# The mean squares and the prompt's attention in the free PSUM columns of the score tiles, in a hybrid backbone step on one Trainium2 core

## The chip, the cores and the metric

The kernel runs on one core of a Trainium2 chip. The metric is the device time of one execution in microseconds (us). The five engines of a core each work through a program of their own, in order: PE (TensorE, matmuls and transposes), DVE (VectorE), ACT (ScalarE), POOL (GpSimd) and SP (SyncE, which here only issues DMAs). Matmul results land in PSUM, which has eight banks of 512 fp32 columns per partition.

## The reference

Two layers of a hybrid backbone with 1,024 sample tokens, 128 prompt tokens and a model width of 1,024. One input projection of each layer yields q, k, v and gate of four attention heads and the inputs of a Fourier and a gMLP branch. The attention is differential and ends in a norm over each head's 128 outputs:

```python
s = einsum('bhqmd,bhkmd->bhmqk', q, k) * HEAD_DIM ** -0.5      # m = 0, 1
p = softmax(s, axis=-1)
a = p[:, :, 0] - lam * p[:, :, 1]
o = einsum('bhqk,bhke->bhqe', a, v)
o = o * rsqrt(mean(o ** 2, axis=-1) + RMS_EPS) * subln_w * (1 - lam_init)
```

Sample queries see 128 cached and 1,024 own keys (1,152 in all); the prompt's 128 queries see the prompt's 128 keys alone. Then `mixed = o * silu(gate)` and the branches go through an output projection and a layer norm.

## The kernel before, in words

**The stages.** Each layer projects its inputs (line 386, PSUM tiles `z`, matmuls of 128x384), works through the attention, the gMLP and the Fourier branch, and ends in the output projection (`y`, line 1013). The attention does not wait for all projections: the projections of later heads and of the branches are cut into small steps and are put between the steps of the attention by the generator `fill`, so that TensorE has work while ACT and DVE do the softmax.

**The attention.** `attention` (line 695) has one iteration per query tile of 128 queries, eight tiles in each of four heads; tile i of head h is step n = 8h + i. An iteration has four steps on TensorE, with projections behind each: the scores for m = 0 and for m = 1 (`score`, line 632: six matmuls into a tile `S`, DVE's maximum `nm` at line 640, ACT's exponential `P` at line 642), every second time the product with the values for two earlier tiles (`values`, line 658: 27 matmuls into `pv`), and the nine transposes of the previous tile's probabilities (`transpose`, line 646: `T`, copied by ACT at line 655 to `a`, the rest of the precision by DVE at line 656). Between scores and transposes, `softmax_diff` (lines 583 to 585) joins both exponentials on DVE and POOL.

**PSUM.** `S`, `T` and `pv` share the tag "S": two slots of three banks each. A score fills columns 0 to 383 of each of its three banks; columns 384 to 511 stay empty. A new tile of this tag takes over the slot of the tile two allocations earlier, once all of that tile's readers are done. All other results (`z`, `vt`, and the prompt's small tiles) share the tag "mm": two slots of one bank.

**The norm.** `values` squares `pv` on ACT (`sq`, line 589). One step of projections later `finish_o` lets TensorE form the mean of the squares (a matmul with a matrix of 1/128, line 594) into the other half of the bank that holds `pv`, DVE multiplies `pv` into `gs` (line 595), ACT reads the mean (`msq`, line 598), takes a logarithm and an exponential (lines 599, 600), POOL multiplies three times (601 to 603), and DVE finishes (604). The slot of `pv` is free after line 598.

**The prompt's attention.** `prompt` (line 670) is a generator of five steps, started after the first `values` of a head and served by a `Stream` at one step per step of the attention: two scores (`sp`, line 678, with a maximum and an exponential `Pp` each, lines 679 and 680), the softmax, a transpose (`atp`, line 685, copied by ACT at 687), the product (`pvp`, line 690) and its norm. Every tile of it takes a slot of the tag "mm", between two `z`.

**The order.** TensorE's order is the order in which the program is written (`manual_schedule`). The other engines are ordered by a scheduler, with the attention's instructions ahead (`high_priority`).

Of the kernel before, what the change touches and what calls it, by code (L numbers as in the profile page):

```python
# [12 lines left out]
AF = mybir.ActivationFunctionType  # L13
ALU = mybir.AluOpType
AX = mybir.AxisListType
# [4 lines left out]
SEQ_S = 1024  # L20
# [10 lines left out]

PACE = 2
SHARE = [0.75, 1.25, 1, 1]
# [17 lines left out]

X_TAGS = {"wr": ("wraw", "woraw", "wada", "tabr", "mr", "ba"), "z": ("zz", "sh", "gt", "vT", "gmt", "gmg", "fot", "vs", "bd", "pqp", "ws", "kc", "vc", "Pp", "modacc"), "Q": ("Q", "bdr", "wsr", "h32"),
          "sq": ("sq", "wft", "dftp", "msq", "bds", "cb")}
X_BUFS = {"wr": 2, "z": 3, "Q": 2, "sq": 3, "X": 2}
# [8 lines left out]
def backbone_step(ctx, tc, xs, xp, cT, w_ada, b_ada, w_in, w_out, ckT, cv, lamv, wf, wsT, bsT,  # L63
# [527 lines left out]

    def finish_o(l, o, ms, sq, n, gs, sl):

        pe.matmul(ms, lhsT=onesm, rhs=sq[:, :n], start=True, stop=True)
        dve.scalar_tensor_tensor(gs[:, sl], o, subs[:, l:l + 1], gs[:, sl], op0=ALU.mult, op1=ALU.mult)

        m = tX([128, 256], "msq")[:, :n]
        act.activation(m, ms, AF.Identity, bias=epsr)
        act.activation(sq[:, :n], m, AF.Ln)
        act.activation(sq[:, :n], sq[:, :n], AF.Exp, scale=-0.5)  # L600
        pool.tensor_tensor(m, m, sq[:, :n], op=ALU.mult)
        pool.tensor_tensor(m, m, sq[:, :n], op=ALU.mult)
        pool.tensor_tensor(gs[:, sl], gs[:, sl], sq[:, :n], op=ALU.mult)
        dve.scalar_tensor_tensor(gs[:, sl], m, 3.0, gs[:, sl], op0=ALU.subtract, op1=ALU.mult)


    class Head:
# [23 lines left out]

        def score(self, Q, i, m, zz):
            S, K = psS(), self.K
            ql = slice((i % 2) * 128, (i % 2) * 128 + 128)

            for e, q in enumerate((Q[:, m, ql], qlo[i % 2][:, m])):
                for n in range(3):
                    pe.matmul(S[:, n, :CH], lhsT=q, rhs=K[:, m, n * CH:(n + 1) * CH], start=e == 0, stop=e == 1)  # L638
            nm = small([128, 1], "nm", 4)
            dve.tensor_reduce(nm, S[:, :, :CH], axis=AX.XY, op=ALU.max, negate=True)  # L640
            P = tP(name="P")
            act.activation(P.rearrange("p (c k) -> p c k", c=3), S[:, :, :CH], AF.Exp, bias=nm,  # L642
                           accum_out=zz[:, m:m + 1])
            return P

# [12 lines left out]
        def values(self, p):  # L658
            pv = psS((128, 2, 256), "pv")
            for kt in range(NT):  # L660
                for e, (a, b) in enumerate(((0, 0), (0, 1), (1, 0))):
                    pe.matmul(pv[:, 0, :], lhsT=self.V[:, a, kt, :], rhs=self.A[:, b, kt, :],  # L662
                              start=kt == 0 and e == 0, stop=kt == 8 and e == 2)
# [6 lines left out]
        def prompt(self):  # L670

            l = self.l
            nm = small([128, 2], "nmp", 2)
            zz = small([128, 2], "zzp", 2)
            P = tX([128, 2, 128], "Pp")
            for m in range(2):
                S = psM((128, 128), "sp")
                pe.matmul(S, lhsT=self.qp[:, m], rhs=self.kp, start=True, stop=True)
                dve.tensor_reduce(nm[:, m:m + 1], S, axis=AX.X, op=ALU.max, negate=True)
                act.activation(P[:, m], S, AF.Exp, bias=nm[:, m:m + 1], accum_out=zz[:, m:m + 1])  # L680
                yield 0.5 * PACE
            softmax_diff(l, P[:, 0], P[:, 1], zz, "p")
            yield 0.5 * PACE
            pt = psM((128, 128), "atp")
            pe.transpose(pt, P[:, 0], ident)
            aT = P[:, 1]
            act.activation(aT, pt, AF.Copy)
            yield 0.5 * PACE
            pv = psM((128, 2, 128), "pvp")
            pe.matmul(pv[:, 0], lhsT=self.vp, rhs=aT, start=True, stop=True)  # L690
            sq = square_o(pv[:, 0], 128)
            yield 0.5 * PACE
            finish_o(l, pv[:, 0], pv[:, 1], sq, 128, self.gs, slice(SEQ_S, TOK))

    def attention(l, fill):
# [3 lines left out]
        done = None  # L699
        side = Stream()  # L700
        for n in range(8 * H + 2):
            h, i = min(n // 8, H - 1), n % 8
            if n < 8 * H:
                if i == 0:
                    fill.until((l, U_K + h), (l, U_Q + h), (l, U_V + h))
                    hd = Head(l, h)
                    Qn = hd.pack(0)
# [8 lines left out]
                with tc.high_priority(offset=EARLY):  # L716
                    side.fill(1)
# [5 lines left out]
                with tc.high_priority(offset=EARLY):  # L723
                    side.fill(1)
                yield h, 1
            if done:
                if done[1] == 0:
                    fill.until((l, U_G + done[0].h))
                    done[0].begin_values()
                with tc.high_priority(offset=EARLY):  # L730
                    finish = done[0].values(done[1])
                with tc.high_priority(offset=EARLY):
                    side.fill(1)
                yield h, 2
                with tc.high_priority(offset=EARLY):
                    finish()
                if done[1] == 0:
                    side.gens.append(done[0].prompt())
                if done[1] == 3:
                    with tc.high_priority(offset=EARLY):  # L740
                        side.drain()
                    done[0].store()
                done = None
            if turn:
# [5 lines left out]
                turn = None  # L750
                with tc.high_priority(offset=EARLY):
                    side.fill(1)
                yield h, 3
            if n < 8 * H:
                with tc.high_priority(offset=EARLY):
                    softmax_diff(l, p1, p2, zz, "s")
                turn = hd, i, p1

    TG = [[0, 1], [2, 3], [4, 5], [6, 7], [8]]
# [394 lines left out]
```

## Time and profile before

| | us |
|---|---|
| three runs | 1438.85, 1442.42, 1443.56 |
| their median | 1442.42 |
| the profiled execution, its own time | 1439.59 |
| its span, first to last instruction | 1437.7 |
| PE busy | 1330.9 (93%) |
| POOL, DVE, ACT busy | 793.4 (55%), 907.6 (63%), 746.6 (52%) |
| mean granted TensorE clock | 0.979 |

The span is cut by the program into stages. The attention of layer 0 lies between 96 and 580 us (the heads begin at 96, 191, 294 and 412), that of layer 1 between 807 and 1,262 us. A busy share says how much of the time an engine was at work; a wait says how long it stood and whose signal it got last. A timeline row is one instruction, or a run of like ones, with its start and its length, and, in brackets, how long the engine had stood before it.

### The profile page before, as it was taken

Reading aid. Unit: us, or ns where it says so; the run is one execution under the profiler, and the core shown is the slowest. Engines: PE = TensorE matmul, PEld = TensorE weight load, DVE = VectorE, ACT = ScalarE, POOL = GpSimd, SP = SyncE. Lnnn points to the kernel's source line nnn. Section 1 sums busy time; section 2 is a strip of 40 time slices with the busy share of each in tenths; the row PEclk is TensorE's granted clock in tenths of the full one; section 3 lists DMA queues with packets and bytes.
Section 4 is the critical chain, followed back from the end, with each engine's and each line's share of the span. In section 5 each row is a group of like instructions: output and inputs, shape, how many; then the busy total and the mean of one; then the engine's idle time right before and its main releaser. Section 6 shows DMA issues by size and latency. Waiting matters only on the chain. (4 is left out here: it accounts for less than half of the span.)

```text
span 1437.7 us, 21298 instructions
## 1 busy us (share of the span) xinstructions
PE 1330.9 (93%) x8264; PEld 1236.6 (86%) x8264; DVE 907.6 (63%) x1354; ACT 746.6 (52%) x1380; POOL 793.4 (55%) x723
## 2 busy tenths in 40 slices
PE   6899998889899999999997989989799999999997
PEld 4689998879788998987887989988789999998786
DVE  3646667787877865355785565668775684435576
ACT  3576666557454444353656565755565544435320
POOL 2455657567563446336687676575575343533752
PEclk9999999999999999999999999999999999999999
DMA  9310102211220221363341100112020010126432
GB/s 337 147 49 17 35 18 65 75 46 36 88 76 22 98 74 42 108 211 114 124 161 45 50 19 32 49 44 80 32 65 3 30 47 30 47 78 221 154 133 80
DMA packets 56158, 114.43 MB, mean 80 GB/s; under 512 B 4973, under 2 KB 32493, under 8 KB 55929
## 3 DMA queue, kind: packets, MB, share of 16 engines
q1 hardware_dynamic: 56056, 113.07, 23.7%
q8 instruction: 65, 1.06, 0.3%
q14 instruction: 37, 0.30, 0.1%
HBM read 95.47 MB, written 17.58 MB: 79 GB/s over the span
## 5 line engine op out<-in xcount | busy, mean ns | idle before, releaser
L386 PE MATMUL z<-H,w 128*128 128x384 f32 x2520 | 499.8, 345 | 22.4 <-DVE V L506 5.0
L386 PEld LDWEIGHTS z<-H,w 128*128 128x128 f32 x2520 | 444.9, 193 | 29.0 <-ACT vT L492 4.9
L642 ACT ACTIVATE P<-S,nm 128x1152 f32<-128x1152 f32 x128 | 156.4, 1222 | 118.6 <-DVE nm L640 112.1
L640 DVE TENSOR_REDUCE nm<-S 128x1 f32<-128x1152 f32 x128 | 172.3, 1349 | 40.4 <-PE S L638 39.9
L401 PE MATMUL zt<-whi,H 128*128 128x256 f32 x1152 | 158.7, 285 | 4.8 <-ACT ug L767 3.4
L401 PEld LDWEIGHTS zt<-whi,H 128*128 128x128 f32 x1152 | 147.0, 192 | 7.5 <-ACT ug L767 4.0
L584 POOL TENSOR_SCALAR P<-P,rz,neglam 128x1152 f32<-128x1152 f32 x64 | 86.8, 1356 | 98.3 <-DVE rz L583 87.2
L585 DVE SCALAR_TENSOR_TENSOR P<-P,rz 128x1152 f32<-128x1152 f32 x64 | 105.2, 1643 | 42.3 <-POOL P L584 42.3
L630 POOL TENSOR_TENSOR qlo<-qr,Q 64x128 fp32r<-64x128 f32 x128 | 81.4, 641 | 86.8 <-PE S L638 80.2
L367 POOL TENSOR_TENSOR w<-wraw,w 128x1024 fp32r<-128x1024 f32 x36 | 89.6, 2489 | 65.4 <-ACT w L366 64.9
L638 PE MATMUL S<-K,Q 128*128 128x384 f32 x384 | 93.2, 351 | 21.4 <-DVE a L656 11.0
L662 PE MATMUL pv<-a,V 128*128 128x256 f32 x864 | 109.2, 283 | 3.1 <-ACT P L642 3.1
L662 PEld LDWEIGHTS pv<-a,V 128*128 128x128 f32 x864 | 106.6, 191 | 5.1 <-ACT P L642 5.1
L656 DVE TENSOR_TENSOR a<-T,a 128x1152 fp32r<-128x1152 f32 x64 | 86.6, 1353 | 37.5 <-ACT a L655 37.4
L638 PEld LDWEIGHTS S<-K,Q 128*128 128x128 f32 x384 | 67.6, 194 | 29.8 <-DVE a L656 12.8
L638 PE MATMUL S<-K,qlo 128*128 128x384 f32 x384 | 89.7, 342 | 0.0
L1013 PE MATMUL y<-wob,mx 128*128 128x512 f32 (+1 forms) x342 | 88.3, 385 | 1.5 <-DVE rr L1015 1.5
L655 ACT ACTIVATE a<-T 128x1152 fp32r<-128x1152 f32 x64 | 72.3, 1130 | 28.5 <-PE T L652 28.2
L406 PE MATMUL zt<-wlo,H 128*128 128x256 f32 x576 | 82.7, 284 | 1.1 <-POOL wlo L367 1.1
L1013 PE MATMUL y<-wo,mx 128*128 128x512 f32 (+1 forms) x342 | 81.6, 382 | 0.0
L652 PE MATMUL T<-cs,P 128*128 128x128 f32 x576 | 73.9, 274 | 3.8 <-ACT P L642 3.7
L406 PEld LDWEIGHTS zt<-wlo,H 128*128 128x128 f32 x576 | 74.9, 191 | 1.5 <-POOL wlo L367 1.5
(222 smaller groups left out, 2376.9 us busy)
## 6 DMA issues: line engine op xcount, KB each, us to landing
wraw<-in_w_in_dram SPq DMA_DIRECT2D x52, 512.0 KB, 3.3
wada<-in_w_ada_dram SPq DMA_DIRECT2D x32, 512.0 KB, 3.6
wa<-in_w_ada_dram SPq DMA_DIRECT2D x8, 1024.0 KB, 13.0
woraw<-in_w_out_dram SPq DMA_DIRECT2D x16, 512.0 KB, 3.9
mr<-mix SPq DMA_DIRECT2D x18, 384.0 KB, 3.2
mix<-gs SPq DMA_DIRECT2D x8, 576.0 KB, 3.9
x<-rr SPq DMA_DIRECT2D x9, 512.0 KB, 3.6
xr<-x SPq DMA_DIRECT2D x9, 512.0 KB, 5.3
```

Of the source, the lines that this page charges most:

```text
L367: eng.tensor_tensor(lo, raw, f(hi), op=ALU.subtract)
L386: pe.matmul(z, lhsT=w[:, a, kt, :], rhs=Hc[c][:, b, kt, :], start=n == 0, stop=n == 23)
L401: pe.matmul(z[:, i, :], lhsT=Hc[c][:, a, kt, o:o + 128], rhs=w[0][:, kt, :], start=n == 0, stop=False)
L406: pe.matmul(z[:, i, :], lhsT=Hc[c][:, 0, kt, o:o + 128], rhs=w[1][:, kt, :], start=False, stop=kt == KT - 1)
L584: pool.tensor_scalar(p2, p2, rz[:, 1:2], neglam[:, l:l + 1], op0=ALU.mult, op1=ALU.mult)
L585: return dve.scalar_tensor_tensor(p1, p1, rz[:, 0:1], p2, op0=ALU.mult, op1=ALU.add)
L638: pe.matmul(S[:, n, :CH], lhsT=q, rhs=K[:, m, n * CH:(n + 1) * CH], start=e == 0, stop=e == 1)
L640: dve.tensor_reduce(nm, S[:, :, :CH], axis=AX.XY, op=ALU.max, negate=True)
L642: act.activation(P.rearrange("p (c k) -> p c k", c=3), S[:, :, :CH], AF.Exp, bias=nm, accum_out=zz[:, m:m + 1])
L656: dve.tensor_tensor(lo, T[:, :, 0:3], f(hi), op=ALU.subtract)
L662: pe.matmul(pv[:, 0, :], lhsT=self.V[:, a, kt, :], rhs=self.A[:, b, kt, :], start=kt == 0 and e == 0, stop=kt == 8 and e == 2)
L1013: pe.matmul(z, lhsT=mx[:, a, k, :], rhs=wo[kt][b][:, ns], start=i == 0, stop=i == 23)
```

## The change

Four things are written differently.

- The mean of the squares no longer shares the bank of `pv`. `values` now only squares `pv` and multiplies it into `gs` (`begin_o`); it returns `norm`, and the next iteration's first score calls it behind its six matmuls with the free columns of its tile, `S[:, :, 384:]` (`aside`). The mean is two matmuls of 128 columns, in two banks (`mean_o`). The rest of the norm (`finish_o`) follows behind that score's exponential.
- The prompt's attention is a table of four steps, {2: scores, 4: turn, 5: product, 6: norm}: in iteration i of its head the step's matmuls go into the free columns of the second score's tile, and what reads them follows behind that score's exponential. Both score matmuls, one maximum over both, both exponentials and `softmax_diff` are one step. No tile of the prompt takes a slot of the tag "mm" any more, and `Stream`'s part in it and `PACE` are gone.
- The buffer `Pp` in SBUF moves from the group of `z`'s buffers to that of `sq`.
- The store of a head's `gs` to DRAM is issued one step later, behind the last norm.

```diff
-    def finish_o(l, o, ms, sq, n, gs, sl):
-
-        pe.matmul(ms, lhsT=onesm, rhs=sq[:, :n], start=True, stop=True)
+    def begin_o(l, o, n, gs, sl):
+
+        sq = square_o(o, n)
         dve.scalar_tensor_tensor(gs[:, sl], o, subs[:, l:l + 1], gs[:, sl], op0=ALU.mult, op1=ALU.mult)
+        return sq
+
+    def mean_o(free, sq, n):
+
+        for t in range(n // 128):
+            pe.matmul(free[:, t], lhsT=onesm, rhs=sq[:, t * 128:(t + 1) * 128], start=True, stop=True)
+        return free[:, 0:n // 128]
+
+    def finish_o(ms, sq, n, gs, sl):
+
         m = tX([128, 256], "msq")[:, :n]
-        act.activation(m, ms, AF.Identity, bias=epsr)
+        act.activation(m.rearrange("p (t k) -> p t k", k=128), ms, AF.Identity, bias=epsr)
...
-        def score(self, Q, i, m, zz):
+        def score(self, Q, i, m, zz, aside=None):
...
+            after = aside(S[:, :, CH:]) if aside else None
             nm = small([128, 1], "nm", 4)
             dve.tensor_reduce(nm, S[:, :, :CH], axis=AX.XY, op=ALU.max, negate=True)
...
+            if after:
+                after()
             return P
...
         def values(self, p):
-            pv = psS((128, 2, 256), "pv")
+            pv = psS((128, 256), "pv")
...
-            sq = square_o(pv[:, 0], 256)
-            return lambda: finish_o(self.l, pv[:, 0], pv[:, 1], sq, 256, self.gs, slice(p * 256, (p + 1) * 256))
+            sl = slice(p * 256, (p + 1) * 256)
+            sq = begin_o(self.l, pv, 256, self.gs, sl)
+
+            def norm(free):
+                ms = mean_o(free, sq, 256)
+                return lambda: finish_o(ms, sq, 256, self.gs, sl)
+
+            return norm
...
         def prompt(self):
...
+            def scores(free):
+                P = self.P = tX([128, 2, 128], "Pp")
+                for m in range(2):
+                    pe.matmul(free[:, m], lhsT=self.qp[:, m], rhs=self.kp, start=True, stop=True)
+
+                def after():
...
+                    dve.tensor_reduce(nm, free[:, 0:2], axis=AX.X, op=ALU.max, negate=True)
+                    for m in range(2):
+                        act.activation(P[:, m], free[:, m], AF.Exp, bias=nm[:, m:m + 1], accum_out=zz[:, m:m + 1])
+                    softmax_diff(self.l, P[:, 0], P[:, 1], zz, "p")
+                return after
+
+            def turn(free):
+                pe.transpose(free[:, 0], self.P[:, 0], ident)
+
+                return lambda: act.activation(self.P[:, 1], free[:, 0], AF.Copy)
...
+            return {2: scores, 4: turn, 5: product, 6: norm}
...
-                    p1 = hd.score(Q, i, 0, zz)
+                    p1 = hd.score(Q, i, 0, zz, norm and norm[0])
+                    if norm and norm[1]:
+                        norm[1].store()
+                    norm = None
...
-                    p2 = hd.score(Q, i, 1, zz)
+                    p2 = hd.score(Q, i, 1, zz, side.get(i))
```

Three places show how the instructions move. The listings give one engine's program in order; line numbers of the change are those of its own file, in which the projections' line 386 is 385, the scores are 648, the transposes 665 and the exponential 653.

TensorE, head 1 of layer 0, from the last transposes ahead of tile 2 to tile 2's second score, before:

```order
L386 MATMUL z<-H_485,w_1681 128x384 x9
L594 MATMUL pv<-sq,cs 128x256
L652 MATMUL T<-cs,P 128x128 x9
L386 MATMUL z<-H_485,w_1681 128x384 x9
L638 MATMUL S<-K,Q 128x384 x3
L638 MATMUL S<-K,qlo_104 128x384 x3
L386 MATMUL z<-H_485,w_1681 128x384 x6
L638 MATMUL S<-K,Q 128x384 x3
L638 MATMUL S<-K,qlo_104 128x384 x3
L386 MATMUL z<-H_121,w_1859 128x384 x12
```

and now:

```order
L665 MATMUL T<-cs,P 128x128 x9
L385 MATMUL z<-H_485,w_1679 128x384 x9
L648 MATMUL S<-K,Q 128x384 x3
L648 MATMUL S<-K,qlo_104 128x384 x3
L600 MATMUL S<-sq,cs 128x128 x2
L385 MATMUL z<-H_485,w_1679 128x384 x6
L648 MATMUL S<-K,Q 128x384 x3
L648 MATMUL S<-K,qlo_104 128x384 x3
L696 MATMUL S<-kp,qp_107 128x128 x2
L385 MATMUL z<-H_121,w_1857 128x384 x12
```

The mean (line 594 before, 600 now) has gone from behind the projections, ahead of the transposes, to behind tile 2's first score. The prompt's two scores (line 696) stand behind tile 2's second score; before they came later, the first of them behind the transposes that follow tile 3's scores.

ACT, head 1 of layer 0, tile 2: its two exponentials (642 before, 653 now), the gate's three passes (`gt`), the cached keys (`K<-kc`) and the copy of the transposes (`a`), before:

```order
L414 ACTIVATE gt<-z 128x384
L366 ACTIVATE w_2398<-wraw 128x1024
L642 ACTIVATE P,zz_2000<-S,nm 128x1152
L415 ACTIVATE gt<-gt 128x384
L439 ACTIVATE K<-kc 64x128 x2
L642 ACTIVATE P,zz_2000<-S,nm 128x1152
L416 ACTIVATE gt<-gt 128x384
L655 ACTIVATE a<-T 128x9x128
L424 ACTIVATE zz<-z 128x384
```

and now:

```order
L413 ACTIVATE gt<-z 128x384
L365 ACTIVATE w_2384<-wraw 128x1024
L653 ACTIVATE P,zz_1988<-S,nm 128x1152
L607 ACTIVATE msq<-S,epsr 128x256
L414 ACTIVATE gt<-gt 128x384
L438 ACTIVATE K<-kc 64x128 x2
L653 ACTIVATE P,zz_1988<-S,nm 128x1152
L608 ACTIVATE sq<-msq 128x256
L415 ACTIVATE gt<-gt 128x384
L668 ACTIVATE a<-T 128x9x128
L609 ACTIVATE sq<-sq 128x256
L703 ACTIVATE Pp,zzp<-S,nmp 128x128 x2
```

The norm's three instructions (607 to 609) have come in between the two exponentials and behind them, and the prompt's two exponentials (703) stand last, behind the copy of the transposes.

DVE, the start of head 2 of layer 0, from the maximum of step 16's second score to that of the next score (`nm`), with the join of step 16's probabilities (`P`, 585 before, 584 now) and the rest of step 15's transposes (`a`, 656 before, 669 now), before:

```order
L640 TENSOR_REDUCE nm<-S 128x1
L190 SCALAR_TENSOR_TENSOR macc<-wada,csil,macc 128x1024
L433 TENSOR_TENSOR qr<-zz,sh 128x256
L583 RECIPROCAL rz<-zz_2771 128x2
L585 SCALAR_TENSOR_TENSOR P<-P,rz 128x1152
L656 TENSOR_TENSOR a<-T,a 128x9x128
L640 TENSOR_REDUCE nm<-S 128x1
L417 TENSOR_TENSOR gs<-z,gt 128x384
```

and now:

```order
L651 TENSOR_REDUCE nm<-S 128x1
L432 TENSOR_TENSOR qr<-zz,sh 128x256
L582 RECIPROCAL rz<-zz_2758 128x2
L669 TENSOR_TENSOR a<-T,a 128x9x128
L651 TENSOR_REDUCE nm<-S 128x1
L584 SCALAR_TENSOR_TENSOR P<-P,rz 128x1152
L416 TENSOR_TENSOR gs<-z,gt 128x384
```

`a` and the next maximum have moved ahead of `P`; a pass over the modulation (`macc`, line 190) stands elsewhere.

## Rows read from the trace of the kernel before

**Rows 1.** The page's part 1: busy time of each engine, its share of the span, and its instructions.

```profile
PE 1330.9 (93%) x8264; PEld 1236.6 (86%) x8264; DVE 907.6 (63%) x1354; ACT 746.6 (52%) x1380; POOL 793.4 (55%) x723
```

**Rows 2.** The waits of TensorE's queue in the whole span: who waits, for whom, us in total, times, the longest.

```profile
PE atp L685 <- DVE rz L583: 6.4, 4, 2.3
PE atp L685 <- ACT P L642: 2.0, 2, 1.0
PE z L386 <- ACT Pp L687: 2.9, 2, 1.5
PE z L386 <- ACT Pp L680: 2.8, 4, 1.2
PE zt L401 <- ACT Pp L680: 1.5, 1, 1.5
PE S L638 <- ACT msq L598: 5.0, 3, 2.4
PE S L638 <- DVE a L656: 11.0, 3, 4.8
PE pv L662 <- ACT P L642: 3.1, 6, 0.5
```

**Rows 3.** Timeline of TensorE in head 1 of layer 0, two of the waits, and one in head 1 of layer 1 (start us, us, engine, line, operation, out<-in and shapes, count, in brackets the idle time before it and who ended it).

```profile
245.60 0.30 PE L685 MATMUL atp<-cs,Pp 128*128 128x128 f32 x1 [2.31 <-DVE rz L583]
245.66 1.84 PE L386 MATMUL z<-H,w 128*128 128x384 f32 x9
...
265.19 1.33 PE L638 MATMUL S<-K,Q 128*128 128x384 f32 x3 [2.43 <-ACT msq L598]
...
954.75 0.44 PE L685 MATMUL atp<-cs,Pp 128*128 128x128 f32 x1 [2.33 <-DVE rz L583]
954.85 3.23 PE L386 MATMUL z<-H,w 128*128 128x384 f32 x9
```

**Rows 4.** Timeline of ACT in head 1, from the exponential of the first score of tile 2 to the copy of the transposes.

```profile
216.31 1.21 ACT L642 ACTIVATE P<-S,nm 128x1152 f32<-128x1152 f32 x1
...
217.50 0.52 ACT L415 ACTIVATE gt<-gt 128x384 f32<-128x384 f32 x1
217.92 0.64 ACT L439 ACTIVATE K<-kc 64x128 fp32r<-64x128 f32 x2
218.58 1.23 ACT L642 ACTIVATE P<-S,nm 128x1152 f32<-128x1152 f32 x1
...
220.20 1.13 ACT L655 ACTIVATE a<-T 128x1152 fp32r<-128x1152 f32 x1
```

**Rows 5.** Timeline of TensorE around tile 3 of the heads 0, 1 and 2 of layer 0, its first score and what waits behind it; the last row is tile 3's second score in head 0 of layer 1.

```profile
119.67 0.79 PE L638 MATMUL S<-K,Q 128*128 128x384 f32 x3
...
123.78 0.79 PE L638 MATMUL S<-K,Q 128*128 128x384 f32 x3 [1.75 <-ACT P L642]
...
220.45 0.68 PE L638 MATMUL S<-K,Q 128*128 128x384 f32 x3
...
226.85 3.50 PE L662 MATMUL pv<-a,V 128*128 128x256 f32 x27 [0.53 <-ACT P L642]
...
333.36 0.68 PE L638 MATMUL S<-K,Q 128*128 128x384 f32 x3
...
834.47 0.79 PE L638 MATMUL S<-K,Q 128*128 128x384 f32 x3 [1.75 <-ACT P L642]
```

**Rows 6.** Groups of instructions by line and shape (line, engine, operation, names and shapes, count, busy us, mean ns, idle before).

```profile
L680 ACT ACTIVATE Pp<-sp,nmp 128x128 f32<-128x128 f32 x16 | 5.8, 360 | 0.0
...
L680 ACT ACTIVATION_READ_ACCUMULATOR Pp<-sp,nmp 128x1 f32 x16 | 3.2, 201 | 0.0
...
L598 ACT ACTIVATE msq<-pv,epsr 128x256 f32<-128x256 f32 x32 | 15.2, 474 | 41.5 <-DVE gs L595 41.4
...
L600 ACT ACTIVATE sq<-sq 128x256 f32<-128x256 f32 x32 | 13.4, 418 | 0.7
...
L594 PE MATMUL pv<-sq,cs 128*128 128x256 f32 x64 | 19.1, 379 | 0.0
```

**Rows 7.** Timeline of ACT and of TensorE in head 1: the copy of the transposes in iteration 4, and the second score of tile 5.

```profile
243.54 1.14 ACT L655 ACTIVATE a<-T 128x1152 fp32r<-128x1152 f32 x1
...
249.64 0.68 PE L638 MATMUL S<-K,Q 128*128 128x384 f32 x3
```

**Rows 8.** Timeline of ACT, DVE and TensorE at the start of head 2.

```profile
307.10 1.11 ACT L655 ACTIVATE a<-T 128x1152 fp32r<-128x1152 f32 x1
...
308.37 3.49 DVE L585 SCALAR_TENSOR_TENSOR P<-P,rz 128x1152 f32<-128x1152 f32 x1 [1.70 <-POOL P L584]
311.79 1.34 DVE L656 TENSOR_TENSOR a<-T,a 128x1152 fp32r<-128x1152 f32 x1
...
313.19 1.33 PE L638 MATMUL S<-K,Q 128*128 128x384 f32 x3 [4.76 <-DVE a L656]
```

**Rows 9.** The granted TensorE clock by stretch (us, TensorE's busy us and instructions, the clock, the DMA share, GB/s).

```profile
124.90:127.20 2.30, 2.30 (x10) 0.55 0.00 0
313.00:316.00 3.00, 2.81 (x9) 0.50 0.10 37
834.40:837.00 2.60, 2.53 (x14) 1.00 0.02 6
```

**Rows 10.** A wait of ACT's queue in the whole span, columns as in rows 2.

```profile
ACT msq L598 <- DVE gs L595: 41.4, 23, 5.3
```

More of the change, by code (lines that the diff above doesn't have):

```diff
@@ L48 @@
 U_Q, U_K, U_V, U_G, U_F, U_GF, U_U, U_VM, U_GM = 0, 4, 8, 12, 16, 18, 20, 22, 24
-X_TAGS = {"wr": ("wraw", "woraw", "wada", "tabr", "mr", "ba"), "z": ("zz", "sh", "gt", "vT", "gmt", "gmg", "fot", "vs", "bd", "pqp", "ws", "kc", "vc", "Pp", "modacc"), "Q": ("Q", "bdr", "wsr", "h32"),
-          "sq": ("sq", "wft", "dftp", "msq", "bds", "cb")}
+X_TAGS = {"wr": ("wraw", "woraw", "wada", "tabr", "mr", "ba"), "z": ("zz", "sh", "gt", "vT", "gmt", "gmg", "fot", "vs", "bd", "pqp", "ws", "kc", "vc", "modacc"), "Q": ("Q", "bdr", "wsr", "h32"),
+          "sq": ("sq", "wft", "dftp", "msq", "bds", "cb", "Pp")}
 X_BUFS = {"wr": 2, "z": 3, "Q": 2, "sq": 3, "X": 2}
@@ L670, in prompt @@
         def prompt(self):
[L672 to L693, printed above, removed]
+            sl = slice(SEQ_S, TOK)
@@ new lines, in scores @@
+            def scores(free):
[3 more added lines that the diff above has]
+                def after():
+                    nm = small([128, 2], "nmp", 2)
+                    zz = small([128, 2], "zzp", 2)
+                    dve.tensor_reduce(nm, free[:, 0:2], axis=AX.X, op=ALU.max, negate=True)
[3 more added lines that the diff above has]
+                return after
@@ new lines, in turn, with product, after, norm @@
+            def turn(free):
+                pe.transpose(free[:, 0], self.P[:, 0], ident)
+                return lambda: act.activation(self.P[:, 1], free[:, 0], AF.Copy)
+            def product(free):
+                pe.matmul(free[:, 0], lhsT=self.vp, rhs=self.P[:, 1], start=True, stop=True)
+                def after():
+                    self.sq = begin_o(self.l, free[:, 0], 128, self.gs, sl)
+                return after
+            def norm(free):
+                ms = mean_o(free, self.sq, 128)
+                return lambda: finish_o(ms, self.sq, 128, self.gs, sl)
@@ L706, in attention @@
                     hd = Head(l, h)
+                    side = hd.prompt()
                     Qn = hd.pack(0)
@@ L712, in attention @@
                 with tc.high_priority(offset=EARLY):
-                    p1 = hd.score(Q, i, 0, zz)
+                    p1 = hd.score(Q, i, 0, zz, norm and norm[0])
+                    if norm and norm[1]:
+                        norm[1].store()
+                    norm = None
                 if i < 7:
                     hd.low(i + 1, Qn)
-                with tc.high_priority(offset=EARLY):
-                    side.fill(1)
                 yield h, 0
                 with tc.high_priority(offset=EARLY):
-                    p2 = hd.score(Q, i, 1, zz)
+                    p2 = hd.score(Q, i, 1, zz, side.get(i))
                 if i % 2 == 0 and i < 6:
                     Qn = hd.pack(i // 2 + 1)
-                with tc.high_priority(offset=EARLY):
-                    side.fill(1)
                 yield h, 1
+            elif norm:
+                norm[0](psS()[:, :, CH:])()
+                norm = None
             if done:
@@ L730, in attention @@
                 with tc.high_priority(offset=EARLY):
-                    finish = done[0].values(done[1])
-                with tc.high_priority(offset=EARLY):
-                    side.fill(1)
+                    norm = done[0].values(done[1]), done[0] if done[1] == 3 else None
                 yield h, 2
[L735 to L742, printed above, removed]
                 done = None
@@ L750, in attention @@
                 turn = None
-                with tc.high_priority(offset=EARLY):
-                    side.fill(1)
                 yield h, 3
@@ L757, in attention @@
                 turn = hd, i, p1
+        norm[0](psS()[:, :, CH:])()
+        norm[1].store()
     TG = [[0, 1], [2, 3], [4, 5], [6, 7], [8]]
```

4 lines of the change are left out of this document (1 added, 3 removed).

## The prediction

> **What bounds the kernel now.** I read the busy times first: TensorE is at work for 93% of the span, no other engine for more than 63% [rows 1]. Projections fill the attention, so only what TensorE waits for, and a lower clock, can be won or lost. So the second view is its list of waits [rows 2]. The third is the timeline around those waits, for their size one by one and for the clock behind them [rows 3]. The fourth is ACT's timeline at tile 2, where the prompt's exponentials now stand [rows 4].
>
> **What the change removes.** The prompt's small tiles make TensorE wait for what reads them: for the join before the transpose 6.4 and 2.0 us, for the copy 2.9, for the exponentials 2.8 and 1.5 [rows 2]. Together 15.6 us. The norm's `msq` holds the slot of `pv` and the next score waits 5.0 us for it [rows 2]. None of these sixteen waits has a reader left in the new order: the prompt's results now stand a whole iteration ahead of the matmul that takes them up, and `pv` is free once it is squared and multiplied. **Minus 20.6.** This is an upper bound for what goes; its lower bound is zero, if ACT and DVE are late anyway.
>
> **What it costs TensorE.** The 32 means are two matmuls of 128 columns in place of one of 256: as many columns, and I take nothing; the bound is that the whole 19.1 us [rows 6] stood on the way, see the third rival. The prompt's matmuls are the same as before.
>
> **The new wait.** Tile 2's second score now also holds the prompt's scores, so its slot comes free only behind both prompt exponentials. The first score of tile 3 takes over that slot. In ACT's new order these two stand last. I walk head 1 with the durations of before: the first exponential ends at 217.5 [rows 4], `msq` takes 0.47 [rows 6], the gate's pass 0.52, the cached keys 0.64, the second exponential 1.23 [rows 4] and the read of its accumulator 0.2 [rows 6], with the overlaps that the rows have, so 220.4; `sq` 0.42, the gate 0.52, the copy of the transposes 1.13, `sq` again 0.42 [rows 4, 6], so about 222.9; two prompt exponentials at 0.36 + 0.20 [rows 6] end near 224.2. TensorE would be there at 220.45 [rows 5], or 220.75 with the mean and the prompt's scores ahead: a wait of 3.45. The same walk gives 3.75 in head 0, where TensorE is there at 119.67, and 3.2 in head 2, there at 333.36 [rows 5]. In head 3 long projections stand between, and I take none. That is 10.4 us per layer, **plus 20.8**; the bounds are zero, if the scheduler's order leaves ACT ahead of my walk, and about 28, if each is 1.2 us longer for one more copy of 1.13 in front.
>
> What waited behind that place is covered by it then: the 1.75 at tile 3's second score in head 0, in both layers [rows 5], and 0.53 in front of `values` [rows 5] in heads 1 and 2 of both: **minus 5.6**.
>
> **Behind it in head 1.** The copy of the transposes in iteration 4 ends at 244.7 before [rows 7]. It now stands behind the prompt's copy and the norm's last pass, while TensorE, no longer held at 245.60 [rows 3], wants its slot for tile 5's second score 3.6 us sooner than 249.64 [rows 7]. I find 1.8 us of wait there, and by the same walk 0.6 twice just before: 3.0 per layer, **plus 6.0**, between zero and twice that.
>
> **The start of head 2.** There the second score of step 17 waits 4.76 us for the rest of the transposes, which DVE does behind a join of 3.49 us [rows 8]. In the new order it goes ahead of the join. ACT's copy ends at 308.2 [rows 8]; it too is later now, since `msq`, one pass and a product of the modulation stand in front of the exponential ahead of it: I get 308.6, with DVE's 1.34 [rows 8] 309.9, against 313.13. So 3.3 us less, in both layers, where the wait is alike (the longest in [rows 2] is 4.8): **minus 6.6**, between zero and 9.5, all of both waits.
>
> **The clock.** Behind a wait the granted clock sometimes falls to its lower level: 0.50 and 0.55 of 2.4 GHz behind a wait of 4.76 and one of 1.75, but 1.00 behind the other 1.75 [rows 5, 8, 9]. Nine projections took 3.23 us behind a 2.33 and 1.84 behind a 2.31 [rows 3]: 1.4 to 1.6 us for each fall. Two falls go with the waits removed (behind 2.43 and 2.33 [rows 3]), and two at head 2's start may go with the shorter wait; against that, five of the six new waits come where the clock stayed up, and all of them are longer than the waits of 1.75 and 2.3 behind which it once fell and once stayed. 5 x 1.5 - 3.0 - 3.0: **plus 1.5**, between minus 6 and plus 7.5.
>
> **What costs nothing.** ACT's wait of 41.4 us for DVE at `msq` [rows 10] goes; ACT is busy for 52% [rows 1], and none of that wait but the 5.0 above reaches TensorE. `Pp` takes one of three buffers that `sq` and `msq` use: those of the pair before are free some 226, and the next `pv` is done near 231, 4 us behind its start at 226.85 [rows 5]; without that cover a norm would start late, which only the last store feels. The store of `gs` is issued one step later, on SP, past loads of weights; its readers come after the gMLP and Fourier stages. POOL gets no more work; the join of the prompt's 128 columns still goes past its rotations, and its result is wanted two iterations later.
>
> **The sum.** -20.6 + 20.8 - 5.6 + 6.0 - 6.6 + 1.5 = -4.5 on the profiled execution's 1439.6, so 1435.1. The median of the three runs lies 2.8 above that execution, so I forecast **1438.0 us** against 1442.4. A measurement of this kernel can tell about 0.3%, 4.3 us, from no change; the sum stands on that line.
>
> **A rule against it.** The trace has ACT wait 41.4 us, 23 times, for DVE although the two read different columns of one bank [rows 10]. The Trainium skill, "PSUM — Partial Sum Buffer", section "PSUM bank collisions raise a hardware error", says that two engines have to be kept apart in a bank and the same 32 partitions, reads among themselves and disjoint columns included; the trace's wait agrees. By that rule the free columns are free in space, not in time: the score's maximum cannot start before the mean is written, and the slot is held until the mean is read. By it alone the sum would be up to 19.1 us worse; that is the third rival.
>
> **Rivals.**
> - *No slot wait.* If ACT reaches the prompt's exponentials before TensorE wants the slot (because it lost its waits at `msq`), the 20.8 and most of the clock's 7.5 fall away, and the 5.6 stays as it was: -20.6 + 6.0 - 6.6 - 6.0 = -27.2, so 1415.2; the 6.0 taken off last are the falls of the clock that go. For it: ACT is only half busy [rows 1]. Against it: seven instructions in a row stand between the second exponential's start and the end, all of known length. Chance 0.2.
> - *The slot wait wins: slower.* Tile 2's slot holds TensorE six times for more than 3 us, the clock falls each time, and since ACT runs late from there, the copy at head 2's start is late too and `msq` is waited for elsewhere. Then -20.6 + 5.0 + 20.8 - 5.6 + 6.0 + 7.5 - 3.0 = +10.1, so 1452.5. It decides once a wait is longer than some 4.2 us, six times 0.75 above my walk being the 4.5 of the sum. For it: TensorE has no other cover there, its order is fixed. Chance 0.2.
> - *The means on the way.* If the score's chain of maximum, exponential and free slot is what TensorE next waits for at a third of the 32 tiles, a third of 19.1 us comes on top: +6.4, so 1444.3, no change. For it: the 41.4 us that two readers of one bank are kept apart now [rows 10]. Against: between a first score and the next transposes lie projections. Chance 0.17.
>
> **How the numbers follow.** The forecast's own case has 0.43; it lies between 1431 and 1446, half on each side of the line: 0.23 faster, 0.20 same. The first rival adds 0.2 to faster, the second 0.2 to slower, the third 0.13 to same and 0.04 to slower. Together 0.43 faster, 0.33 same, 0.24 slower. The range leaves out the end of the first rival and the end of the second: 1419 to 1451.
>
> **What would show it.** In the profile of the changed kernel: no wait for `Pp`, `atp` or `msq` in TensorE's list; six waits of 3 to 4 us at line 648 for ACT's `Pp` (line 703), in heads 0 to 2 of both layers; head 2's 4.8 us down to about 1.5; a lower clock just behind the six. The forecast is wrong if those six are missing or below 1 us (then the first rival), or if ACT's copy or `msq` becomes the longest wait for scores (the second).

## The result and the profile after

The changed kernel takes 1449.1 us (median of 11 runs, 1441.18 to 1456.97), the kernel before 1440.07 in the same comparison: a ratio of 1.0066 with a 95% interval of 1.0041 to 1.009. It is 0.7% **slower**. The forecast was 1438.0, a little faster. The time lies inside the range of 1419 to 1451, on the other side of no change. In two of the experiments below, e5 and e6, one execution ran at a far lower clock (0.70 and 0.66); the ratios leave it out, the medians don't.

The profiled execution of after took 1452.09 us, 3.0 above that median, with a span of 1450.3 and a mean granted clock of 0.971 (before 1439.59, 1437.7 and 0.979). The first line of its page, against [rows 1]:

```profile
PE 1341.5 (92%) x8328; PEld 1248.1 (86%) x8328; DVE 909.9 (63%) x1346; ACT 741.1 (51%) x1380; POOL 785.7 (54%) x723
```

The span grew by 12.6 us. TensorE is idle for 108.8 us instead of 106.8, so hardly longer; it is *busy* for 10.6 us longer. Its added instructions don't explain that: all means together, the prompt's among them, are this group by line and shape (count, busy us, mean ns, idle before), against 19.1 us [rows 6] and another 3.1 for the prompt's before.

```profile
L600 PE MATMUL S<-sq,cs 128*128 128x128 f32 x144 | 23.4, 282 | 0.0
```

That is 1.2 us. The lower clock more than accounts for the rest, by an estimate from the two pages: 1341.5 x (1 - 0.971) = 38.9 us against 1330.9 x (1 - 0.979) = 27.9, 11.0 more. So the waits that left were replaced by others of nearly the same total, and in this execution more work runs at the lower level behind the new ones. It is one of the slower ones: the median clock of the 11 executions is 0.974, at which the same product is 34.9 us, 7 more than before. The waits of TensorE's queue, against [rows 2] (us in total, times, longest):

```profile
PE S L648 <- ACT Pp L703: 13.5, 6, 2.9
PE S L648 <- ACT P L653: 10.6, 4, 3.0
...
PE vt L498 <- ACT vT L491: 7.5, 2, 3.8
PE zt L400 <- DVE gmg L416: 6.6, 2, 3.3
PE S L648 <- DVE a L669: 6.3, 8, 1.4
...
PE T L665 <- ACT msq L607: 3.0, 2, 1.5
PE S L648 <- ACT msq L607: 2.8, 2, 2.6
```

The waits for `atp` and for the prompt's small tiles are gone, as forecast, and the six waits for `Pp` are there. Two of the large lines were in no walk of the prediction: `vt` for `vT` and `zt` for `gmg`.

**The six slot waits.** TensorE and ACT in the timeline, around tile 3's first score in heads 0, 1 and 2 of layer 0, and ACT ahead of head 1's (columns as in [rows 3]):

```profile
126.08 0.79 PE L648 MATMUL S<-K,Q 128*128 128x384 f32 x3 [2.86 <-ACT Pp L703]
230.83 0.79 PE L648 MATMUL S<-K,Q 128*128 128x384 f32 x3 [1.93 <-ACT Pp L703]
338.75 0.79 PE L648 MATMUL S<-K,Q 128*128 128x384 f32 x3 [1.93 <-ACT Pp L703]
...
227.85 0.19 ACT L653 ACTIVATION_READ_ACCUMULATOR P<-S,nm 128x1 f32 x1
...
228.66 1.12 ACT L668 ACTIVATE a<-T 128x1152 fp32r<-128x1152 f32 x1
...
230.57 0.21 ACT L703 ACTIVATION_READ_ACCUMULATOR Pp<-S,nmp 128x1 f32 x1
```

ACT's order is the one walked. From the end of the second exponential's read (228.04) to the end of the prompt's last read (230.78) it takes 2.7 us; the walk had 3.8, from 220.4 to 224.2. I added lengths that overlap, and the walk's own terms end at 224.0 (222.9 and twice 0.56), not at 224.2.

**The first surprise: `vT`.** One stretch of layer 0, head 0, tiles 5 and 6, all engines of the same timeline (start, length, engine, line, operation):

```profile
153.17 4.41 DVE L613 SCALAR_TENSOR_TENSOR gs<-msq,gs 128x256 f32<-128x256 f32 x1 [0.74 <-POOL msq L611]
153.52 2.39 POOL L366 TENSOR_TENSOR w<-wraw,w 128x1024 fp32r<-128x1024 f32 x1
...
156.56 0.73 POOL L430 TENSOR_TENSOR zz<-zz,rp 128x256 f32<-128x256 f32 x1
...
157.50 1.35 DVE L651 TENSOR_REDUCE nm<-S 128x1 f32<-128x1152 f32 x1
...
158.95 1.22 ACT L653 ACTIVATE P<-S,nm 128x1152 f32<-128x1152 f32 x1 [4.50 <-DVE nm L651]
...
160.72 1.41 DVE L432 TENSOR_TENSOR zz<-zz,sh 128x256 f32<-128x256 f32 x1
...
163.04 0.49 ACT L491 ACTIVATE vT<-z 128x384 f32<-128x384 f32 x1
...
163.59 0.90 PE L498 MATMUL vt<-cs,vT 128*128 128x128 f32 x3 [3.76 <-ACT vT L491]
```

Read it from the top. The last instruction of the norm (line 613, a pass of 0.41 us where nothing disturbs it) now stands ahead of the maximum of tile 5's second score. It takes 4.41 us while POOL works beside it without a pause, and ends at 157.58, just behind POOL's first pause (157.29). That POOL holds it is read from such rows (last section); no run took POOL's work away. The maximum starts at 157.50 (152.21 before), the exponential at 158.95, the rotation of the keys behind it, ACT's copies after that, and TensorE stands for 3.76 us. Layer 1 shows the same, 3.73 at 874.85.

**The second: `gmg`.** DVE and TensorE at the end of layer 1's attention:

```profile
1250.67 1.36 DVE L669 TENSOR_TENSOR a<-T,a 128x1152 fp32r<-128x1152 f32 x1 [4.59 <-ACT a L668]
1251.95 2.73 DVE L366 TENSOR_TENSOR wlo<-wraw,whi 128x1024 fp32r<-128x1024 f32 x1
1254.61 1.24 DVE L416 TENSOR_TENSOR gmg<-zt,gmt 128x512 f32<-128x512 f32 x2
...
1255.43 1.20 PE L400 MATMUL zt<-whi,H 128*128 128x256 f32 x4 [3.32 <-DVE gmg L416]
...
1257.27 2.13 PE L665 MATMUL T<-cs,P 128*128 128x128 f32 x9
```

`gmg`, which frees the bank that the next projection wants, stands behind `a` and a pass over weights; before, it was the first of the three (1245.04). Both layers wait 3.3 us.

**The clock.** Seven stretches of TensorE behind such waits (us, busy and instructions, clock, DMA share, GB/s), as in [rows 9]:

```profile
126.10:129.00 2.90, 2.90 (x17) 1.00 0.54 181
163.60:169.00 5.40, 5.40 (x21) 0.50 0.01 3
340.00:343.00 3.00, 3.00 (x11) 0.50 0.00 0
835.20:838.00 2.80, 2.80 (x9) 0.50 0.56 187
874.90:880.00 5.10, 5.10 (x25) 0.67 0.01 3
1050.00:1053.00 3.00, 3.00 (x11) 0.50 0.00 0
1255.50:1259.30 3.80, 3.80 (x18) 0.50 0.84 309
```

Behind the waits of 3.76 and 3.32 the granted clock is 0.50, the lower of the two levels. Of the six slot waits, three are followed by it: the third and the sixth, 1.93 us each (rows at 340 and 1050), and the fourth, 2.88 (row at 835.2); behind the first, 2.86, the clock stayed at 1.00. The 5.4 us at 163.6 alone hold 2.7 us of that loss: the wait for `vT` costs some 6 us, not 3.8. In layer 1 it is 3.73 and 5.1 x (1 - 0.67) = 1.7 behind it, so some 12 us in both.

### The profile page after: what moved, and what is told of

The parts are those of the page before. It is cut to its first block, busy times and chain, and to the rows that moved or that the text cites. A ratio compares the mean times of both kernels' runs of the same rounds, so it can differ in the third digit from the quotient of the medians.

```text
span 1450.3 us, 21446 instructions
## 1 busy us (share of the span) xinstructions
PE 1341.5 (92%) x8328; PEld 1248.1 (86%) x8328; DVE 909.9 (63%) x1346; ACT 741.1 (51%) x1380; POOL 785.7 (54%) x723
## 4 chain that ended last, share of the span: by engine, by line
PE 38%; DVE 10%; ACT 6%; POOL 4%; issue 3%; DMA 3%; SPq 0%; DVEq 0%; POOLq 0%; ACTq 0%
PE y L1036 10%; PE z L385 7%; PE zt L400 6%; PE zt L405 3%; PE pv L675 3%; PE S L648 3%; ACT P L653 2%; DVE nm L651 2%; PE dft L946 2%; PE T L665 1%; DMA wada<-in_w_ada_dram 1%; DVE rr L1053 1%; DVE rr L1039 1%; POOL zz L430 1%; DVE bns L203 1%
## 5 line engine op out<-in xcount | busy, mean ns | idle before, releaser
L651 DVE TENSOR_REDUCE nm<-S 128x1 f32<-128x1152 f32 x128 | 172.2, 1349 | 42.1 <-PE S L600 19.7
L583 POOL TENSOR_SCALAR P<-P,rz,neglam 128x1152 f32<-128x1152 f32 x64 | 91.1, 1423 | 95.0 <-DVE rz L582 95.0
L648 PE MATMUL S<-K,Q 128*128 128x384 f32 x384 | 93.5, 352 | 34.1 <-ACT Pp L703 13.5
L639 POOL TENSOR_TENSOR qlo<-qr,Q 64x128 fp32r<-64x128 f32 x128 | 74.7, 588 | 92.8 <-PE S L648 77.8
L584 DVE SCALAR_TENSOR_TENSOR P<-P,rz 128x1152 f32<-128x1152 f32 x64 | 108.2, 1691 | 18.4 <-POOL P L583 18.4
L610 POOL TENSOR_TENSOR msq<-msq,sq 128x256 f32<-128x256 f32 (+1 forms) x40 | 35.9, 896 | 96.2 <-ACT sq L609 93.5
L665 PE MATMUL T<-cs,P 128*128 128x128 f32 x576 | 77.0, 281 | 3.0 <-ACT msq L607 3.0
## 6 DMA issues: line engine op xcount, KB each, us to landing
wa<-in_w_ada_dram SPq DMA_DIRECT2D x8, 1024.0 KB, 13.1
```

What stands on the lines that cost most here:

```text
L583: pool.tensor_scalar(p2, p2, rz[:, 1:2], neglam[:, l:l + 1], op0=ALU.mult, op1=ALU.mult)
L584: return dve.scalar_tensor_tensor(p1, p1, rz[:, 0:1], p2, op0=ALU.mult, op1=ALU.add)
L665: pe.transpose(T[:, kt // 3, kt % 3, :], a[:, kt * 128:(kt + 1) * 128], ident)
```

## The experiments

Two questions: do the two surprises carry the loss (theory), or the six slot waits (the prediction's own, and its second rival)? And which half of the change brings them? Each ratio is to the kernel before on the same chip.

**e1: the norm's last pass behind the maximum.** Head 0's first norm of each layer reads a constant that is computed from the second score's maximum, so line 613 can't be put ahead of it. All else is the change.

```diff
-        dve.scalar_tensor_tensor(gs[:, sl], m, 3.0, gs[:, sl], op0=ALU.subtract, op1=ALU.mult)
...
+            dve.tensor_scalar(three, nm, 0.0, 3.0, op0=ALU.mult, op1=ALU.add)
+            dve.scalar_tensor_tensor(gs[:, sl], m, three, gs[:, sl], op0=ALU.subtract, op1=ALU.mult)
```

> The changed kernel with one instruction moved: in head 0 of each layer, DVE's last step of the first norm (gs<-msq) is tied to the maximum of tile 5's second score, by a scalar computed from it, so that it stands behind that maximum and not ahead of it. My theory: in the changed kernel this step runs 4.41 us instead of 0.42, because POOL works without a pause beside it, and the maximum, ACT's exponential, the copy vT and TensorE's vt wait for it (3.76 us in layer 0, and as much in layer 1), with a lower granted clock behind; the two places cost 6.2 and 5.2 us against the kernel before. Moved, the wait falls to about 1 us and the clock stays up: 8 to 11 us less than the 1449 of the changed kernel, so 1438 to 1441. Rival: vT is late because the prompt's square and K's halves stand ahead of it on ACT; then the wait stays at 3 to 4 us and the time at 1449.

Measured: 1435.99 us, ratio 0.9983 (0.996 to 1.0007). One instruction of 0.41 us per layer, moved behind one maximum, takes 0.8% off the change's time: 13 us by the medians, somewhat more than the 8 to 11 expected. In the trace all other instructions of TensorE, DVE, ACT and POOL stand in the change's order. TensorE's wait for `vT` is no longer in the list. DVE in the same stretch:

```profile
151.18 2.72 DVE L659 TENSOR_REDUCE nm<-S 128x1 f32<-128x1152 f32 x2
...
154.20 3.47 DVE L620 SCALAR_TENSOR_TENSOR gs<-msq,three,gs 128x256 f32<-128x256 f32 x1
...
157.91 0.41 DVE L432 TENSOR_TENSOR zz<-zz,sh 128x256 f32<-128x256 f32 x1
```

The pass is still held (3.47 us), but both maxima are out ahead of it, and the rotation starts at 157.91 instead of 160.72. So the first surprise is shown: nothing else was moved.

**e2: the tail's order.** The last transposes go behind the projections that follow them, and POOL takes the low half of the Fourier unit's weights, so that `gmg` comes early.

```diff
+                if n == 8 * H - 1:
+                    yield h, 3
                 with tc.high_priority(offset=EARLY):
...
-                yield h, 3
+                if not (n == 8 * H - 1):
+                    yield h, 3
...
-            load_unit(..., dve if j else pool)
+            load_unit(..., dve if j and u != U_F else pool)
```

> The changed kernel with the end of each attention rearranged: in step 31 the transposes stand behind the projections that follow them and not ahead, and the low half of the Fourier unit's second weights is made by POOL and not by DVE, so that DVE reaches the gate's product gmg without the rest of the transposes (1.36 us) and that pass (2.73 us) ahead of it. My theory: in the changed kernel gmg waits behind these two, TensorE stands 3.32 us for the slot that gmg reads, at the end of both attentions, and runs at a lower granted clock behind: 4.6 us in layer 0, part of which the output projection's own waits take in, and 6 us in layer 1. Without it 6 to 10 us less than the 1449 of the changed kernel, so 1439 to 1443, and no wait of zt for gmg over 1 us. Rival: TensorE is only early there, and waits next for the weights or the transposes as long; then the time stays within 2 us of 1449.

Measured: 1443.95 us, ratio 1.0031 (1.0009 to 1.0054); no wait for `gmg` in its list. It takes some 0.35% off, 5 us by the medians: less than the 6 to 10 expected, and barely clear of the noise of the two ratios.

**e3: the prompt's steps one tile later.** This takes away the slot waits, since tile 3 is followed by a product with the values.

```diff
-            return {2: scores, 4: turn, 5: product, 6: norm}
+            return {3: scores, 5: turn, 6: product, 7: norm}
```

> The changed kernel with the prompt's four steps at tiles 3, 5, 6 and 7 in place of 2, 4, 5 and 6. At an odd tile the product with the values takes the next slot, and the slot of the second score is taken up only by the transposes behind it, some 9 us later, so that both prompt exponentials are read long before. My theory: the six waits of scores for Pp (13.5 us in all) go; waits that they covered come back (1.75 twice in head 0, 0.5 four times before the values), so 5 to 9 us less than 1449, 1440 to 1444, unless the scheduler's order moves something else. Rival: these waits only stand in place of others, since ACT and DVE are the slower ones from tile 2 to tile 4; then waits of the same sum appear at the scores of tiles 3 and 4, and the time stays at 1449.

Measured: 1453.84 us, ratio 1.01 (1.007 to 1.013), a miss. The waits for `Pp` are gone, and this stands in their place in TensorE's list:

```profile
PE S L648 <- ACT P L653: 32.8, 11, 5.8
```

The longest of these, in the timeline of DVE and TensorE in head 1:

```profile
222.86 2.00 DVE L184 TENSOR_SCALAR macc<-wada,csil 128x1024 f32<-128x1024 f32 x2 [1.24 <-DMA wada<-in_w_ada_dram]
224.79 1.87 DVE L584 SCALAR_TENSOR_TENSOR P<-P,rz 128x1152 f32<-128x1152 f32 x1
226.58 1.34 DVE L651 TENSOR_REDUCE nm<-S 128x1 f32<-128x1152 f32 x1
...
229.33 1.33 PE L648 MATMUL S<-K,Q 128*128 128x384 f32 x3 [5.84 <-ACT P L653]
```

Two passes over the modulation, for which no instruction waited, stand ahead of the join and a maximum, and themselves wait for a DMA. None of these is an instruction that the table moves: the scheduler's order put them so. e6 below shows the same wait.

**e4: e1, e2 and e3 together.** The edits are those three, one line of each:

```diff
+            dve.scalar_tensor_tensor(gs[:, sl], m, three, gs[:, sl], op0=ALU.subtract, op1=ALU.mult)
...
+                if n == 8 * H - 1:
...
+            return {3: scores, 5: turn, 6: product, 7: norm}
```

> The three edits of the runs before together: the first norm's last step behind the maximum, the end of the attention rearranged, and the prompt's steps at tiles 3, 5, 6 and 7. If the three costs are separate and are all that turned the change from a gain to a loss, the sum is 1449 - 10 - 8 - 7 = 1424, between 1418 and 1430, so 10 to 20 us less than the kernel before. If TensorE only moves on to the next engine's wait, it stays above 1436.

Measured: 1443.47 us, ratio 1.0026 (1.0005 to 1.0048), a miss, with e3's eleven waits for the exponential again (32.9 us, the longest 5.8).

**e5: e1 and e2 without e3.** One line of each:

```diff
+            dve.scalar_tensor_tensor(gs[:, sl], m, three, gs[:, sl], op0=ALU.subtract, op1=ALU.mult)
...
+                if n == 8 * H - 1:
```

> The first two edits together, with the prompt's steps where the change has them (tiles 2, 4, 5, 6). Alone, the first made the changed kernel 13 us faster (1449 to 1436) and the second 5 us (to 1444). They stand some hundred us apart and touch different instructions, so I expect the sum, 1431, between 1427 and 1436, and 4 to 13 us less than the kernel before. The waits of vt for vT and of zt for gmg should both be gone, the six waits for Pp (13.5 us) still there. Rival: the second edit's gain is taken in by later waits once TensorE comes earlier; then 1436.

Measured: 1434.17 us, ratio 0.9956 (0.9938 to 0.9973), as expected. The waits for `vT` and `gmg` are gone from the list, the six waits for `Pp` are all there, 13.5 us, and the kernel is faster than before. So the two surprises, 1.1% together, are more than the whole loss, and the slot waits are not what made the change slow.

**e6: the norms' half alone.** The mean goes into the score's free columns; the prompt stays as before. Two lines of the edit, against the changed kernel:

```diff
-                    p2 = hd.score(Q, i, 1, zz, side.get(i))
+                    p2 = hd.score(Q, i, 1, zz)
...
+                        side.gens.append(done[0].prompt())
```

> Half of the change: the mean squares of the sample tiles go into the first score's free columns, one iteration later, and the prompt's attention stays in its own small tiles, as before. In DVE's order the norm's last step stands between the two maxima of tile 5 in head 0 again, and gmg behind the rest of the transposes and the weights' pass at the end of the attention. My theory: both surprises of the change come from this half. Then vt waits 2 to 4 us for vT twice, zt 3.3 us for gmg twice, no score waits for Pp, and the prompt's 15.6 us of waits are there as before: 1440 - 5.0 + 11 + 5 to 10, so 1451 to 1456. Rival: the contention in head 0 needs the prompt's steps too; then 1440 to 1446.

Measured: 1455.85 us, ratio 1.011 (1.0087 to 1.0132). The time came as expected, the waits only in part: `zt` waits for `gmg` (7.7 us), but no `vt` for `vT`. DVE has the norm's last pass between the two maxima of tile 5 here too; it starts at 149.19 and is held for 2.39 us only. In TensorE's list:

```profile
PE S L649 <- ACT P L654: 21.4, 7, 5.9
PE T L666 <- ACT msq L608: 14.1, 4, 6.6
```

DVE's timeline at the start of head 2 of layer 0:

```profile
300.80 3.71 DVE L190 SCALAR_TENSOR_TENSOR macc<-wada,csil,macc 128x1024 f32<-128x1024 f32 x2 [0.49 <-DMA wada<-in_w_ada_dram]
304.42 2.69 DVE L433 TENSOR_TENSOR qr<-zz,sh 128x384 f32<-128x384 f32 x1
307.04 1.34 DVE L652 TENSOR_REDUCE nm<-S 128x1 f32<-128x1152 f32 x1
```

The transposes take over a score's slot that now is free only when `msq` has been read, and `msq` stands behind an exponential whose maximum began at 307.04. This is the wait of 6.6 in the list. It is not the norms' alone: e7 below, with the norms as before, waits 6.05 us at the same transposes, for the exponential. The longest wait of a score is this one, in head 1:

```profile
230.30 1.33 PE L649 MATMUL S<-K,Q 128*128 128x384 f32 x3 [5.85 <-ACT P L654]
```

It stands at the first score of tile 3, as e3's 5.84, and behind the same two passes over the modulation. Both kernels have the means in the score tiles and no prompt step at tile 2; so e3's wait needs no step at tile 3.

**e7: the prompt's half alone.** The norms stay as before, the table of steps and `Pp`'s place are those of the change. Two lines of the edit, against the kernel before:

```diff
+                    side = hd.prompt()
...
-                    p2 = hd.score(Q, i, 1, zz)
+                    p2 = hd.score(Q, i, 1, zz, side.get(i))
```

> The other half: the prompt's attention goes into the second score's free columns at tiles 2, 4, 5 and 6, and the mean squares of the sample tiles stay beside pv, as before. DVE's order has the norm's last step behind both maxima of tile 5, and gmg ahead of the weights' pass at the end. My theory: TensorE loses the prompt's 15.6 us of waits, gets six waits of about 2 us for Pp, and loses the 5.6 us that these cover; msq is waited for as before, some 5 us. So 1440 - 15.6 + 13.5 - 5.6, 1432, between 1427 and 1440; no wait of vt for vT and none of zt for gmg over 1 us. Rival: the slot waits bring a lower clock with them; then 1440 or more.

Measured: 1418.63 us, ratio 0.9857 (0.9836 to 0.9879): 1.4% **faster**, 21 us where 8 were expected and the range ended at 13, and better than both kernels. TensorE is idle for 9.6 us less than before and busy for 9.3 less (1321.6 us, at a granted clock of 0.982). Its two largest waits within the attention:

```profile
PE T L658 <- ACT P L646: 15.8, 4, 6.3
PE S L641 <- ACT Pp L690: 9.7, 6, 2.9
```

The slot waits of heads 1 and 2 are 0.99 us each here, where the change has 1.93; there two passes of the norm (lines 608 and 609, 0.41 us each) stand ahead of the prompt's exponentials on ACT.

**e8 and e9: the prompt's half in other tiles.**

```diff
-            return {2: scores, 4: turn, 5: product, 6: norm}
+            return {3: scores, 5: turn, 6: product, 7: norm}      # e8
+            return {1: scores, 3: turn, 5: product, 6: norm}      # e9
```

> The prompt's half alone (the norms as before), its steps now in the tiles {3: scores, 5: turn, 6: product, 7: norm}. Tile 3 is the last in front of a product with the values, so its slot isn't wanted by a score at once. If the slot waits are a price of their own, the 9.7 us of six waits for Pp go and part of the clock behind them: 1405 to 1413. The rival: the scheduler's new order makes another maximum late, as it did when the whole change had these steps (eleven waits for the exponential, 32.8 us): then 1420 to 1435, with waits of 3 to 6 us at tile 3's second score.

> The prompt's half alone (the norms as before), its steps in the tiles {1: scores, 3: turn, 5: product, 6: norm}. The slot waits move from tile 3's first score to tile 2's. If what counts is that the prompt no longer shares the bank of the projections, any such table gains: 1414 to 1428, with six waits for Pp of 1 to 3 us at tile 2. The rival, that the place of the steps decides through the order of DVE and ACT, says that it may lose the whole gain: over 1430, with a wait of more than 3 us that the first table doesn't have.

Measured: e8 1427.8 us, ratio 0.992 (0.9895 to 0.9945), e9 1418.07, ratio 0.9844 (0.9807 to 0.988). The waits of e8:

```profile
PE T L658 <- ACT P L646: 12.6, 6, 2.7
PE S L641 <- ACT P L646: 10.9, 6, 3.3
```

Those of e9:

```profile
PE T L658 <- ACT P L646: 16.9, 5, 6.1
...
PE S L641 <- ACT Pp L690: 2.9, 2, 1.4
```

e8 missed its 1405 to 1413 and lies in the rival's range. It has no wait for `Pp` and is slower than e7; other scores wait for exponentials. But its trace does not explain the loss: TensorE is idle for 96.5 us in it and for 97.2 in e7's, and the profiled execution took 4 us less than e8's median. e9 came out as expected in time, with two of the six waits. It has a third of e7's waits for `Pp` and the same time. All three tables beat the kernel before. So the prompt's half gains wherever its steps stand, and the place decides how much; that it does so through the order of DVE and ACT is likely, not shown.

## Why the prediction went wrong

- **What the change removes, minus 20.6.** The prompt's 15.6 us left; the prompt's half alone gains 20.7 us net, slot waits and clock included (e7). The 5.0 for `msq` did not leave: 3.0 + 2.8 are waited for it now, since the mean holds a score's slot instead of that of `pv`.
- **The new wait, plus 20.8.** Right in place and count, too large: 13.5, mostly by the overlaps above.
- **What it covers, minus 5.6.** The 1.75 at tile 3's second score is gone in both layers; the waits ahead of `values` are not (2.8 us instead of 3.1).
- **Head 1, plus 6.0.** Tile 5's second score waits 2.36 and 2.39 us where I had 1.8, for the exponential instead of the copy.
- **Head 2, minus 6.6.** The wait of 4.76 [rows 8] has gone in both layers. A new one, 2.89 and 3.00 us for the exponential, stands at the first score of step 17, but the transposes before it no longer wait. From the first score of step 16 to the second of step 17 the gain is 4.9 and 4.7 us, 9.6 in all, the far end of what I allowed.
- **The clock, plus 1.5.** Measured: 11.0 from the two pages, and 7 at the median clock of the changed kernel's executions, so about the bound of 7.5. Three falls follow slot waits, where I had five; others follow waits that I had not seen.
- **What costs nothing: here the prediction failed.** This part asks only who waits for the results of the moved instructions. It does not ask what they now stand ahead of on their engine, and takes for granted that all else keeps its order. With the norm an iteration later the scheduler put its last pass, line 613, ahead of a maximum, and `gmg` behind a pass over weights. These two waits are 14.1 us (7.5 + 6.6) before the clock; taken away, they give back 1.1% (e5 against the change). Without them the sum of -4.5 comes out: e5's ratio is 6.3 us below the kernel before. That is partly luck. The slot waits were 7.3 us too large, head 2's gain 3.0 too small, and against them `msq` did not leave, the clock cost more, and the two waits ahead of `mres` (2.4 + 2.0 us, hardly any before) were in no term.
- **The rule on PSUM banks and the third rival.** TensorE shows no price for it: the means take 23.4 us against 22.2, and each first score with a mean delays the second by 0.45 us, which the transposes that lost the mean give back. The Trainium skill, "PSUM — Partial Sum Buffer", section "PSUM bank collisions raise a hardware error", says that two engines must be kept apart in a bank and the same 32 partitions. The trace agrees: DVE's maximum, which reads other columns of these banks, waits for the means, 18 times.

  ```profile
  DVE nm L651 <- PE S L600: 19.7, 18, 2.3
  ```

  But what the slot's longer hold costs TensorE is the 5.8 us of waits for `msq` (5.0 before), not 19.1.
- **The second rival** had the right side and nearly the time (1452.5), but by luck: two of its terms came, `msq` waited for elsewhere and a lower clock, and its mechanism did not. The slot waits are shorter than walked, not longer, and head 2 gained.

The two halves alone are -20.7 and +16.5 us, -4.2 together; the change is +9.0. The difference of 13 is about what e1 took off (13.1 us by the medians of the two, measured in different comparisons), and neither half has the wait of `vt` for `vT`. That the two are the same is not shown: e6 loses by other waits than the change, 21.4 us for the exponential and 14.1 for `msq`, where the change has 10.6 and 3.0.

What stays open: why e5 is still some 15 us slower than e7. Of the 11.2 between their spans, idle time explains none (95.2 us against 97.2), busy time all (1334.8 against 1321.6). With the clocks of 0.976 and 0.982, 32.0 - 23.8 = 8.2 of that is the clock. The traces name some places: the clock is 0.50 behind four of e5's six slot waits (three of them of 1.93 or 1.94 us), and behind one of e7's, where heads 1 and 2 wait 0.99. This was not tried one by one.

## What to carry to other kernels

Where a scheduler orders the engines, compare the whole order of every engine, in all stages, before saying that something costs nothing; look first for work that nobody waits for, or a pass that another engine can hold, ahead of an instruction at the head of a chain. Test a change in halves: here one half gains 1.4%, the other loses 1.1%. And count a wait of TensorE at its length plus the slower stretch behind it.

## What the hardware did that I had not expected

A pass of DVE over two SBUF tensors can be held by POOL for far longer than its own work. In the changed kernel the norm's last pass (`gs<-msq,gs`, 128x256) took 0.41 to 0.43 us the ten times that POOL was at work for less than a tenth of it, and up to 4.41 with POOL at work; the join `P<-P,rz` 1.40 to 1.42 in 21 such cases, and up to 3.58 with POOL at work. POOL at work does not always hold it: ten of the other 22 last passes took 0.43 us or less too. The maxima `nm<-S` and the rests `a<-T,a`, which read PSUM, stayed at 1.36 us or less in all 192 cases. The Trainium skill, "SBUF — State Buffer", section "Who interferes with whom", says that a DVE instruction with two SBUF inputs contends with a POOL instruction that reads SBUF, and calls the ports that the two share an exclusive lock. These rows agree on who is held; but the pass of 4.41 us outlasted four POOL instructions in a row (153.10 to 157.29), not one.
